# Mixture-of-experts stage with slots by place: small experts in 32 slots on four column quarters, a float32 gather, and biases added behind the transposes

## The chip, the core and the metric

The kernel runs on one core of one Trainium2 chip. The metric is the device time of one execution in microseconds (us), as the median of several runs; lower is better. One execution is also recorded by the hardware profiler, and its rows are what this document reads.

## The reference, cut to what matters

One layer of a decoder: a token mixer (three attention branches) and then a mixture of 32 experts, over 256 tokens of width 1024, all in float32. The change is in the experts alone. A router picks four experts for each token, and what is computed is

```python
logits = tok @ router_w + router_b
top_v, top_i = lax.top_k(logits, 4)
top_w = softmax(top_v)                       # combine[t, e]: weight or 0
for e in range(32):
    gu = tok @ w_gu[e] + b_gu[e]             # (256, 2048)
    gate = minimum(gu[:, 0::2], 7.0)
    up = clip(gu[:, 1::2], -7.0, 7.0)
    act = (up + 1.0) * (gate * sigmoid(1.702 * gate))
    out = out + combine[:, e:e + 1] * (act @ w_down[e] + b_down[e])
```

The kernel computes an expert only for the tokens that were routed to it. An expert has 2048 columns of gate and up weights and 1024 of down weights, 12 MB in float32, and all 32 are read from HBM once.

## The kernel before

Behind the token mixer the router's logits are turned and the four largest are taken. Then experts are sorted by their number of tokens. **Places**: experts 0 and 1 have places 0 and 1 (FIXED), so that their weights can be loaded ahead of the sort; the others follow by falling number of tokens. Places 2 to 7 are **wide** (up to 128 tokens, class `Wide`), all others **narrow** (up to 64, class `Narrow`). If some place holds more tokens than it has slots, a flag is set, and a branch behind the sweep (L1664) computes what was left out.

**Groups.** Experts come in groups of two members. For a group, `choose` (GpSimd) builds a 0/1 matrix `sel` of tokens by slots; `gather` multiplies tokens with it, so that X holds a group's tokens, transposed, in slots; `slots` turns `sel` into `selT` for the scatter; `weights` gathers the routing weight of each slot into `wsl`. The gather runs in fp32r on two halves of the tokens, `tokh` (rounded) and `tokl` (the rest): eight pieces for a group, four copied into X by ScalarE and four added by VectorE (L1244). `Group.plan` puts these pieces between the steps of the expert ahead.

**Steps.** `sweep` goes through 24 half-steps for each expert, in the order N N N N, then W N N N and so on (N narrow, W wide; the groups are a pair of narrow ones and a wide with a narrow one in turn). Matmuls of weights are float32 with 512 moving columns; X (or the activation) is the loaded operand. A wide expert uses 128 columns of the array. A narrow expert runs two matmuls on the two 64-column halves (`tile_position=(0, 64 * e)`): gate columns go to PSUM rows 0 to 63, up columns to 64 to 127. It does this for each half f of the hidden width: eight X steps of two halves of a copy each, with `part` behind steps 4 and 8, then four steps for down. `part` evicts the PSUM bank to `gu`, turns it by four transposes (L1425), and VectorE and ScalarE make the activation `an` (L1434 to L1440). Biases are added by one more matmul into the same bank, `bgu` times `pick` or `pickN`. `leave` scales y by `wsl` into `yh` and `yl`, and a scatter with `selT` adds it to four PSUM banks `acc`.

**Queues.** Order on TensorE, SyncE and GpSimd is that of the program; each engine goes on when its waits are fulfilled. All weights come over SyncE's queue (`Stream.raw`, L97): copies of 512 KB, 24 for an expert, into a ring of 35 slots (`Stream.slot`), of which 2 * PAIRS lie in a pool of large tiles that `tokh` and `tokl` share. A copy waits until the matmuls that read its slot's earlier content are done.

## Time and profile before

| | before |
|---|---|
| median of 3 runs | 1328.62 us (1326.39 to 1328.7) |
| profiled execution | 1328.49 us |
| its span | 1326.7 us |
| TensorE busy | 1283.1 us (97%) |
| VectorE, ScalarE, GpSimd busy | 33%, 22%, 7% |
| copies | 478.19 MB, mean 360 GB/s over the span |
| first and last copy of expert weights issued | 233.2 us, 1275.3 us |
| first expert matmul | 288.35 us |

The span is the time from the first to the last instruction of the profiled execution. PE is TensorE's matmul and PEld its weight load, DVE VectorE, ACT ScalarE, POOL GpSimd, SP SyncE, SPq the queue of copies that SyncE issues. Every float32 matmul stands in the trace as two passes with a weight load each. Matmul ends are modelled, so that the starts of weight loads are the better clock of TensorE.

### The profile page before, as it was taken

The numbers are of one execution on the slowest core, as the hardware profiler recorded it, in microseconds if no ns is written. First come the engines' busy times: TensorE is split into PE (matmuls) and PEld (weight loads), VectorE is DVE, ScalarE is ACT, GpSimd is POOL, SyncE is SP. The second block draws the span as 40 slices with busy tenths as digits, with TensorE's granted clock in tenths as the row PEclk, the third lists the DMA queues.
The fourth block names the chain that finished last, engine by engine and source line by source line (L and its number), as shares of the span: only waits on it lengthen the run. The fifth ranks groups of instructions, "written<-read, shape, count | busy, mean of one in ns | idle before, by whom it ended". The sixth has DMA issues, their size and how long they took to land. (4 is left out here: it accounts for less than half of the span.)

```text
span 1326.7 us, 18133 instructions
## 1 busy us (share of the span) xinstructions
PE 1283.1 (97%) x6198; PEld 653.3 (49%) x6198; DVE 433.6 (33%) x921; ACT 285.3 (22%) x552; POOL 97.5 (7%) x149
## 2 busy tenths in 40 slices
PE   6999999989999999999999999999999999999993
PEld 6889888863333443344335433543354335343431
DVE  7898788761131111211111121212121112111114
ACT  4555555341111011111111111011101110111112
POOL 0014621010000000000000000000000000000000
PEclk9999999999899999999999999999999999999997
DMA  9998787689999999999999999999999999899970
GB/s 364 352 333 287 267 275 271 222 318 395 408 408 409 409 409 407 406 404 344 411 408 409 319 402 409 408 329 409 409 399 337 409 408 400 315 409 409 407 287 34
DMA packets 134531, 478.19 MB, mean 360 GB/s; under 512 B 16557, under 2 KB 17130, under 8 KB 134432
## 3 DMA queue, kind: packets, MB, share of 16 engines
q1 hardware_dynamic: 132656, 471.66, 92.2%
q0 software_dynamic: 1632, 5.03, 1.1%
q8 instruction: 51, 0.84, 0.3%
q14 instruction: 48, 0.39, 0.1%
q10 hardware_dynamic: 144, 0.26, 0.1%
HBM read 475.82 MB, written 3.44 MB: 361 GB/s over the span
## 5 line engine op out<-in xcount | busy, mean ns | idle before, releaser
L192 PE MATMUL b<-raw,X 128*64 128x512 f32 (+1 forms) x2048 | 563.1, 599 | 0.0
L192 PEld LDWEIGHTS b<-raw,X 128*64 128x64 f32 (+1 forms) x2048 | 178.2, 146 | 268.4 <-issue 248.9
L192 PE MATMUL b<-raw,an 128*64 128x512 f32 (+1 forms) x1024 | 288.2, 606 | 1.2
L192 PEld LDWEIGHTS b<-raw,an 128*64 128x64 f32 (+1 forms) x1024 | 86.7, 147 | 131.8 <-issue 108.9
L192 PE MATMUL b<-hh,hi 128*128 128x256 f32 x336 | 97.9, 291 | 12.6 <-ACT hh L319 12.6
L1434 DVE TENSOR_SCALAR gm<-b 128x256 f32<-128x256 f32 x52 | 22.1, 424 | 234.6 <-PE b L1425 234.6
L192 PE MATMUL b<-hl,hi 128*128 128x256 f32 x336 | 95.9, 286 | 1.8 <-DVE hl L320 1.8
L192 PE MATMUL b<-hh,lo 128*128 128x256 f32 x336 | 95.5, 284 | 0.6 <-DVE lo L157 0.4
L1244 DVE TENSOR_TENSOR X<-b,X 128x256 f32<-128x256 f32 (+1 forms) x60 | 28.6, 477 | 167.8 <-PE b L192 167.8
L1315 DVE SCALAR_TENSOR_TENSOR yl<-b,wsl,yh 128x512 fp32r<-128x512 f32 x38 | 28.5, 751 | 165.8 <-ACT yh L1314 151.4
L1420 ACT ACTIVATE gu<-b 128x512 f32<-128x512 f32 x52 | 31.0, 597 | 199.3 <-PE b L192 199.3
L157 DVE TENSOR_TENSOR lo<-raw,hi 128x1024 fp32r<-128x1024 f32 (+1 forms) x58 | 69.5, 1212 | 11.4 <-ACT hi L146 9.4
L192 PEld LDWEIGHTS b<-hh,hi 128*128 128x128 f32 x336 | 64.0, 191 | 14.4 <-ACT hh L319 12.6
L146 ACT ACTIVATE hi<-raw 128x1024 fp32r<-128x1024 f32 (+1 forms) x58 | 59.8, 1047 | 31.7 <-PE b L192 23.0
L192 PEld LDWEIGHTS b<-hl,hi 128*128 128x128 f32 x336 | 63.7, 190 | 2.8 <-DVE hl L320 2.7
L192 PEld LDWEIGHTS b<-hh,lo 128*128 128x128 f32 x336 | 64.1, 191 | 1.3 <-DVE lo L157 1.0
L1172 POOL TENSOR_SCALAR sel<-cst,pq 128x128 fp32r<-128x128 f32 x48 | 28.1, 600 | 450.7 <-PE b L192 450.7
L1314 ACT ACTIVATE yh<-b,wsl 128x512 fp32r<-128x512 f32 x38 | 26.1, 687 | 153.1 <-PE b L192 153.1
L1242 ACT ACTIVATE X<-b 128x256 f32<-128x256 f32 (+1 forms) x60 | 25.5, 425 | 154.4 <-PE b L192 154.4
L1435 ACT ACTIVATE th<-gm 128x256 f32<-128x256 f32 x52 | 21.6, 416 | 137.9 <-DVE gm L1434 137.9
L192 PEld LDWEIGHTS b<-sel,tokh 128*128 128x128 f32 x240 | 34.0, 190 | 32.6 <-issue 32.0
L192 PEld LDWEIGHTS b<-sel,tokl 128*128 128x128 f32 x240 | 34.3, 193 | 27.7 <-issue 27.3
(321 smaller groups left out, 1242.9 us busy)
## 6 DMA issues: line engine op xcount, KB each, us to landing
raw<-in_wexp SPq DMA_DIRECT2D x768, 512.0 KB, 10.1
raw<-in_modg SPq DMA_DIRECT2D x32, 512.0 KB, 6.0
raw<-in_wmg SPq DMA_DIRECT2D x24, 512.0 KB, 9.5
raw<-in_moda SPq DMA_DIRECT2D x16, 512.0 KB, 8.3
raw<-in_cw SPq DMA_DIRECT2D x8, 512.0 KB, 9.2
raw<-in_wbr SPq DMA_DIRECT2D x8, 512.0 KB, 6.3
raw<-in_wout SPq DMA_DIRECT2D x8, 512.0 KB, 5.8
raw<-in_wg SPq DMA_DIRECT2D x8, 448.0 KB, 8.9
```

Of the source, the lines that this page charges most:

```text
L146: self.nc.scalar.activation(hi[:, :m], src, AF.Copy)
L157: self.nc.vector.tensor_sub(part[2][:, :m], src, hi[:, :m].bitcast(F32))
L192: PE.matmul(out, x, w, start=start, stop=stop, skip_group_check=True, **kw)
L1172: engine.tensor_scalar(sel[:, i].rearrange("p (r j) -> p r j", r=2), C("iota64")[:, None, :].to_broadcast([128, 2, 64]), src[:, i, p:p + 1 ...
L1242: ACT.activation(x, bv, AF.Copy)
L1244: V.tensor_add(x, bv, x)
L1314: return (yh, yl, lambda: ACT.activation(yh, y, AF.Copy, scale=wsl), lambda: V.scalar_tensor_tensor(yl, y, wsl, yh.bitcast(F32), op0=OP.mu ...
L1315: lambda: V.scalar_tensor_tensor(yl, y, wsl, yh.bitcast(F32), op0=OP.mult, op1=OP.subtract))
L1420: at(side, t, lambda: ACT.activation(gu, b, AF.Copy))
L1434: V.tensor_scalar(v(gm), zv[:, :, 0], 7.0, None, op0=OP.min)
L1435: ACT.activation(th[:, 0:256], gm[:, 0:256], AF.Tanh, scale=0.851)
```

## The change

- Three kinds of expert by place: places 2 to 8 wide (128 slots, one more than before), 0, 1 and 9 to 17 narrow (64), 18 to 31 **few** (32 slots, class `Few`). The groups are the two fixed, one narrow pair, and then seven times a wide with a narrow and a pair of few ones: the order is N N N N and seven times N W F F.
- `Few` runs four matmuls on the four 32-column quarters of the array: for the X steps, a quarter each for gate and up of either hidden half; for down, each quarter takes one half of the output for one half of the hidden width, and the scatter adds the two up. A step takes four copies; there are four X steps, one `part` behind them, and two down steps.
- The gather runs in float32 on `h2` itself: four pieces for a group, all copied by ScalarE. `tokh` and `tokl`, their splitting and the additions into X are gone; the ring has a fourth pair of slots (37 in all).
- Biases: `sort_biases` makes a table `biasT` by place (hidden unit on the partition) with 16 small matmuls once, and VectorE adds it to the turned values behind the transposes (`clipped`). The bias matmuls, `bgu`'s split, `pick` and `pickN` are gone. A wide expert now evicts to `gu` and turns gate and up, where it turned the product alone.
- Slot weights are gathered in float32 without a split.
- The flag also looks at place 18, and the branch behind the sweep handles the new kinds.

On TensorE, the second half of a narrow expert stands so before (`raw` is a weight slot, `cst` the identity; the first member after a wide expert):

```order
L192 MATMUL b<-raw,X 64x512 x12
L192 MATMUL b<-bgu,pickN 128x512
L192 MATMUL b<-raw,an 64x512 x4
L1425 MATMUL b<-cst,gu 128x128 x4
L192 MATMUL b<-raw,an 64x512 x12
```

On TensorE in the changed kernel, the second half of a few expert (first of its pair), with a piece of the gather (`sel`, `h`) and the scatter behind it:

```order
L190 MATMUL b<-raw,X 32x512 x16
L1285 MATMUL b<-cst,gu 128x128 x4
L190 MATMUL b<-raw,an 32x512 x16
L190 MATMUL b<-sel,h_3115 128x192 x4
L190 MATMUL b<-yh,selT 128x512 x2
L190 MATMUL b<-yl,selT 128x512 x2
```

Before, down matmuls of the first hidden half stood between the last X matmul and the transposes of the second half; now nothing stands between the last X matmul, the one set of transposes and the first down matmul of a few expert. The bias matmul is gone.

On VectorE, the activation of one narrow half before (its inputs come from the PSUM bank `b`):

```order
L1434 TENSOR_SCALAR gm<-b 128x256
L1436 TENSOR_SCALAR an<-b 128x256
L1437 SCALAR_TENSOR_TENSOR gm<-an,gm 128x256
L1440 SCALAR_TENSOR_TENSOR an<-th,gm 128x256
L1315 SCALAR_TENSOR_TENSOR yl<-b,wsl,yh 128x512
```

On VectorE in the changed kernel, the activation of a whole few expert:

```order
L1269 TENSOR_TENSOR gm<-b,biasT 128x256
L1271 TENSOR_SCALAR gm<-gm 128x256
L1269 TENSOR_TENSOR up<-b,biasT 128x256
L1273 TENSOR_SCALAR up<-up 128x256
L1369 SCALAR_TENSOR_TENSOR gm<-up,gm 128x256
L1372 SCALAR_TENSOR_TENSOR an<-th,gm 128x256
L1280 SCALAR_TENSOR_TENSOR yl<-b,wsl,yh 128x512
```

Six operations stand where four stood, the two additions from the table being new, and they stand once for a few expert, twice for a narrow one.

The diff, cut to its core:

```diff
-HALF = 64
 FIXED = 2
-WIDE = 8
+WIDE = 9
+NARROW = 18
 RAW_BUFS = 10
 LOW_BUFS = 4
 RAW_MORE = 11
-PAIRS = 3
+PAIRS = 4
 AHEAD = 4
...
-                tok = (tokh, tokl)[s]
...
+            def gather(self, t, c2):
+
                 b = ps()
+                n = self.members[0][1]
                 for c in range(2):
                     for i in range(2):
...
+                        sel = self.sel[:, i, 0:self.width]
+                        if len(self.members) == 2 and n < 128:
+                            sel = self.sel[:, i].rearrange("p (s j) -> p s j", s=2)[:, :, 0:n]
+                        mm(b[:, c * self.width:(c + 1) * self.width],
+                           h2[:, i, (2 * c2 + c) * 128:(2 * c2 + c + 1) * 128], sel, i == 0, i == 1)
+                at(side, t + 2, lambda: ACT.activation(
+                    self.X[:, 2 * c2:2 * c2 + 2, 0:self.width],
+                    b[:, 0:2 * self.width].rearrange("p (c w) -> p c w", c=2), AF.Copy))
...
+            def clipped(self, v, z, bias, gate):
+
+                shape = [128, z.shape[1], z.shape[2]]
+                V.tensor_tensor(v, z, bias[:, :, None].to_broadcast(shape), OP.add)
+                if gate:
+                    V.tensor_scalar(v, v, 7.0, None, op0=OP.min)
+                else:
+                    V.tensor_scalar(v, v, 7.0, -7.0, op0=OP.min, op1=OP.max)
 
...
+            def turned(self, gu):
+                z = ps()
+                for j in range(4):
+                    PE.transpose(z[:, j * 128:(j + 1) * 128], gu[:, j * 128:(j + 1) * 128], C("ident"))
+                return z
...
-                        mm(b, self.pick[:, up].to_broadcast([128, 128]), bgu[:, f * 512:(f + 1) * 512], False, True)
...
+                    z = self.turned(gu).rearrange("p (c s) -> p c s", c=4)
+                    bias = biasT[:, self.place, :, f, up]
+
+                    def gate():
+                        self.gm, self.th = t2k("gm", 1), t2k("th", 1)
+                        self.clipped(self.gm.rearrange("p (c s) -> p c s", c=4), z, bias, True)
+                        ACT.activation(self.th, self.gm, AF.Tanh, scale=0.851)
+
+                    def both():
+                        a = self.act[f] = t2k("an", 2)
+                        self.clipped(a.rearrange("p (c s) -> p c s", c=4), z, bias, False)
+                        V.scalar_tensor_tensor(self.gm, a, 1.0, self.gm, op0=OP.add, op1=OP.mult)
+                        V.scalar_tensor_tensor(a, self.th, 1.0, self.gm, op0=OP.add, op1=OP.mult)
+
+                    at(side, t + 2, both if up else gate)
+
+                at(turn, t, turned)
...
+        class Split(Expert):
...
+            def activation(self, z, m, slots, bias, t):
+
+                gm, th, up = t2k("gm", 1), t2k("th", 1), t2k("up", 1)
+                a = t2k("an", 2)
+                z = z.rearrange("p (m e s) -> p m e s", m=m, e=2)
+
+                def v(x):
+                    return x[:, 0:256].rearrange("p (m s) -> p m s", m=m)
+
+                def begin():
+                    self.clipped(v(gm), z[:, :, 0], bias[0], True)
+                    ACT.activation(th[:, 0:256], gm[:, 0:256], AF.Tanh, scale=0.851)
+                    self.clipped(v(up), z[:, :, 1], bias[1], False)
+                    V.scalar_tensor_tensor(gm[:, 0:256], up[:, 0:256], 1.0, gm[:, 0:256], op0=OP.add, op1=OP.mult)
+
+                at(side, t, begin)
+                at(side, t, lambda: V.scalar_tensor_tensor(a[:, 0:256], th[:, 0:256], 1.0, gm[:, 0:256],
+                                                           op0=OP.add, op1=OP.mult))
+                return a
...
-                        mm(b, self.G.pickN[self.slot], bgu[:, f * 512:(f + 1) * 512], False, True)
...
+        class Few(Split):
+
+
+            def step(self, h):
+                r, rest = divmod(h, 4)
+                if rest != 3:
+                    return
+                w = [W.use((self.key, 2 * r + e // 2), e % 2) for e in range(4)]
+                X = self.G.x(self.slot)
+                if r in (0, 4):
+                    self.b = ps()
+                for k2 in range(2):
+                    for e in range(4):
+                        c = 2 * (r % 4) + k2
+                        x = X[:, c] if r < 4 else self.act[0][:, 64 * c + 32 * (e % 2):64 * c + 32 * (e % 2) + 32]
+                        mm(self.b[32 * e:32 * e + 32], x, w[e](k2 * 512, 512), c == 0, c == (7 if r < 4 else 3),
+                           tile_position=(0, 32 * e))
+                if r == 3:
+                    self.part(self.b)
+                elif r == 5:
+                    self.y = self.b
+                    self.leave()
+
+            def part(self, b):
+                t = self.t0 + 16
+                gu = t2k("gu", 1)
+                at(side, t, lambda: ACT.activation(gu, b, AF.Copy))
+
+                def turned():
+                    self.act[0] = self.activation(
+                        self.turned(gu), 8, 32,
+                        [biasT[:, self.place].rearrange("p c f e -> p (c f) e")[:, :, e] for e in range(2)], t + 1)
+
+                at(turn, t, turned)
+
+        KIND = {128: Wide, 64: Narrow, 32: Few}
...
-        tokh = s8([128, 2, D], "tokh", F32R)
-        tokl = s8([128, 2, D], "tokl", F32R)
...
+        biasT = mp.tile([128, 32, 4, 2, 2], F32, name="biasT")
...
+        def sort_biases():
+            for e in range(2):
+                b = ps()
+                rows = slice(32 * e, 32 * e + 32)
+                for c in range(4):
+                    for f in range(2):
+                        k = 2 * c + f
+                        mm(b[:, 32 * k:32 * k + 32], bgu[rows, 512 * f + 128 * c:512 * f + 128 * c + 128], perm[rows],
+                           True, True, tile_position=(32 * e, 0))
+                at(side, 6, lambda e=e, b=b: V.tensor_copy(biasT[:, :, :, :, e].rearrange("p q c f -> p (c f) q"),
+                                                           b[:, 0:256].rearrange("p (k q) -> p k q", k=8)))
 
...
+        def slots_of(p):
+            return 64 if p < FIXED else 128 if p < WIDE else 64 if p < NARROW else 32
+
+        by = {n: [(p, n) for p in range(FIXED, NE) if slots_of(p) == n] for n in KIND}
+        groups = [G0, Group(pq, [by[64].pop(0), by[64].pop(0)])]
+        while by[32]:
+            groups.append(Group(pq, [by[128].pop(0), by[64].pop(0)]))
+            groups.append(Group(pq, [by[32].pop(0), by[32].pop(0)]))
+        assert not any(by.values())
```

## Rows read from the trace of the kernel before

**Rows 1.** The page: busy time, share of the span and count of each engine.

```profile
PE 1283.1 (97%) x6198; PEld 653.3 (49%) x6198; DVE 433.6 (33%) x921; ACT 285.3 (22%) x552; POOL 97.5 (7%) x149
```

**Rows 2.** Table by stretch: busy us per engine, granted clock, DMA share, GB/s.

```profile
290.00:1290.00 1000.00, 998.84 (x4225) 410.31 (x4223) 179.00 (x374) 129.86 (x245) 40.67 (x84) 1.00 1.00 391
420.00:460.00 40.00, 39.92 (x152) 17.33 (x148) 7.48 (x15) 4.11 (x8) 2.55 (x6) 1.00 1.03 409
740.00:780.00 40.00, 39.92 (x180) 15.42 (x180) 6.61 (x14) 5.18 (x9) 2.57 (x5) 1.00 0.96 347
```

**Rows 3.** Waits, copy queue (SPq) and weight loads (PEld): us in total, times, longest.

```profile
SPq L97 <- DMA raw<-in_wexp: 417.6, 562, 2.2
SPq L97 <- PE b L192: 156.0, 187, 3.9
...
PEld b L192 <- DMA raw<-in_wexp: 18.0, 64, 0.8
```

**Rows 4.** Timeline, PEld: first weight load of six experts; start us, us, instruction.

```profile
409.33 0.14 PEld L192 LDWEIGHTS b<-raw,X 128*64 128x64 f32 x2 [0.28 <-issue]
...
484.69 0.20 PEld L192 LDWEIGHTS b<-raw,X 128*64 128x64 f32 x4 [0.36 <-issue]
...
510.21 0.14 PEld L192 LDWEIGHTS b<-raw,X 128*64 128x64 f32 x2 [0.28 <-issue]
...
539.72 0.14 PEld L192 LDWEIGHTS b<-raw,X 128*64 128x64 f32 x2 [0.28 <-issue]
...
566.13 0.30 PEld L192 LDWEIGHTS b<-raw,X 128*128 128x128 f32 x2 [0.81 <-issue]
...
615.11 0.20 PEld L192 LDWEIGHTS b<-raw,X 128*64 128x64 f32 x4 [0.37 <-issue]
```

**Rows 5.** Timeline, PEld, of a narrow expert: a scatter, transposes, plain pairs.

```profile
616.02 0.14 PEld L192 LDWEIGHTS b<-raw,X 128*64 128x64 f32 x2 [0.29 <-issue]
...
618.59 0.14 PEld L192 LDWEIGHTS b<-raw,X 128*64 128x64 f32 x2 [0.29 <-issue]
...
625.82 0.14 PEld L192 LDWEIGHTS b<-raw,X 128*64 128x64 f32 x2 [0.28 <-issue]
626.77 0.42 PEld L1425 LDWEIGHTS b<-cst,gu 128*128 128x128 f32 x4 [0.81 <-issue]
...
627.84 0.14 PEld L192 LDWEIGHTS b<-raw,X 128*64 128x64 f32 x2 [0.29 <-issue]
...
629.13 0.14 PEld L192 LDWEIGHTS b<-raw,X 128*64 128x64 f32 x2 [0.28 <-issue]
629.56 0.14 PEld L192 LDWEIGHTS b<-raw,X 128*64 128x64 f32 x2 [0.28 <-issue]
```

**Rows 6.** Timeline of the same expert: last load, eviction gu, the VectorE chain.

```profile
624.14 0.19 PEld L192 LDWEIGHTS b<-bgu,pickN 128*128 128x128 f32 x1 [0.81 <-issue]
...
624.68 0.60 ACT L1420 ACTIVATE gu<-b 128x512 f32<-128x512 f32 x1 [1.70 <-PE b L192]
...
627.47 0.42 DVE L1434 TENSOR_SCALAR gm<-b 128x256 f32<-128x256 f32 x1 [2.29 <-PE b L1425]
...
628.84 0.43 DVE L1440 SCALAR_TENSOR_TENSOR an<-th,gm 128x256 f32<-128x256 f32 x1
```

**Rows 7.** Copies into raw from 290 us: count, ns, first and last issue; landing.

```profile
L97 SPq DMA_DIRECT2D raw<-in_wexp x739: 327/333/663, 289.9 to 1275.3; - x185
...
DMA to landing us min/median/max: 3.8/10.1/11.9
```

**Rows 8.** Timeline, PEld and ACT: last weight load of the experts, last eviction.

```profile
1303.77 0.14 PEld L192 LDWEIGHTS b<-raw,an 128*64 128x64 f32 x2 [0.29 <-issue]
...
1304.87 0.69 ACT L1314 ACTIVATE yh<-b,wsl 128x512 fp32r<-128x512 f32 x1 [4.70 <-PE b L192]
```

**Rows 9.** TensorE 32-row matmuls (timeline), then the table by stretch right after.

```profile
333.64 4.16 PE L192 MATMUL b<-raw,ppT 32*128 32x512 f32 x8
...
338.00:340.00 2.00, 2.00 (x8) 1.20 (x10) 0.42 (x1) 0.00 (x0) 0.00 (x0) 0.50 1.01 406
```

## The prediction

> **What bounds the kernel now.** I read the page first: TensorE is busy for 97% of the span [rows 1]. Busy is not the same as bound, so I went on to the table by stretch. While the experts run, the copies move 409 GB/s in the good stretches and 347 in a bad one, and 391 as a mean over 290 to 1290 us [rows 2]. So two resources are close to their limit together. The waits say which one ends last: the weight loads of TensorE waited for a copy only 64 times and 18.0 us in total, while the copy queue waited 156.0 us for TensorE to free a slot, in 187 waits [rows 3]. TensorE never starves; the copies are held up by it. (The 417.6 us in which the queue waits for an earlier copy is the ring at work, not a stall.)

> The starts of the experts confirm it [rows 4]. From 484.69 to 615.11 four experts take 25.5 us (narrow), 29.5 (narrow, with eight gathers for the next group), 26.4 (narrow) and 49.0 (wide): 130.4 us. The copies for four experts are 96 of 512 KB, and at 409 GB/s one takes 1.282 us, so 123.1. TensorE loses 7.3 us on the copies in each such period, six of which stand in the program. The **ceiling** of any gain here is therefore the copy stream: what it needs from the point where it is saturated, plus a tail.

> **The terms of the copy stream.** The median time is 1328.62 us; the profiled execution took 1328.49, its span 1326.7, so 1.8 us lie around the span. From 289.9 us on 739 copies are issued [rows 7]. The first 29 are not changed: they wait on work ahead of the experts. Run without a stall, 738 steps of 1.282 us put the last issue at 1236.0 instead of 1275.3; the median landing of 10.1 us, and about 1.5 us for the small copies of rows and biases between them, put the last landing at 1248. That is 39 us gained if TensorE keeps up. Then the tail. Before, the last landing (1275.3 + 10.1, so about 1285) finds TensorE with most of the last expert still to do; its final matmul begins at 1303.77 [rows 8]. In the changed kernel the last expert is a "few" one, whose last step (eight matmuls, four at a time) starts when its copies land. With 0.6 us to start, four passes, and the 1.1 us from the last pass to its eviction [rows 8], the eviction begins 3.0 us after the landing, at 1251 instead of 1304.87. What follows is not changed: 1326.7 - 1304.87 = 21.8 us. The span is then 1272.8.

> **Does TensorE keep up?** It has to do four experts (few, few, narrow, wide) in under 123.1 us.
> - Passes. Every f32 matmul is two passes over 512 columns. Two 64-column matmuls go side by side at 0.43 us a pair of passes [rows 5]. A narrow expert has 48 such pairs, 20.6 us. A few expert has 24 sets of four 32-column matmuls. The trace shows no quarter, so I bound it from both sides: 0.43 us a set (four truly side by side, 10.3 us an expert), 0.86 (two at a time, 20.6) or 1.72 (one at a time, 41). Below 0.43 nothing is possible, since each set streams 512 columns as the pair does. I take 0.43, the value of the nearest row, which shows that halves cost nothing extra.
> - Interruptions. Undivided work between column tiles delays the tiled stream: a scatter takes 618.59 - 616.02 less three normal pairs, 1.28 us; four transposes 0.73 [rows 5]. The first few expert of a pair carries the transposes of the choice, the slot weights (taken like transposes) and one late scatter of the wide one: 2.5 us. The second carries a scatter and four float32 gathers. Eight gathers made the second narrow expert 29.5 us instead of 25.5 less its 1.5 for choice and weights, so eight cost 5.5; the four new ones have as many passes (float32 takes two) and half the interruptions, and I take 4.8, between 2.7 and 5.5.
> - The new stall. A few expert does all its gate and up columns before anything is evicted, and its down matmuls then need all of it. TensorE waits for the eviction of `gu` (0.54 us after the last pass begins, and 0.60 long), the transposes (0.70 until VectorE begins) and a chain of six VectorE operations. Four of them took 1.80 us; the two additions from the bias table add their mean of 0.45 each [rows 5, 6]. Together 4.7 us where 0.43 was normal: 4.3. Queued behind it on TensorE are the down matmuls, and nobody else waits. It is paid only while TensorE is behind the copies; otherwise the next copies are not there yet either (four take 5.1 us).
> - Sum: first few 17.1, second 20.7. Narrow: 26.4 less two bias matmuls (about 0.6 each), plus 0.9 for two more VectorE operations ahead of its last down matmuls: 26.1. Wide: 49.0 less four bias matmuls of 0.43, plus eight more transposes (0.9) and some 0.5 for float32 gathers: 48.7. Together **112.6 us against 123.1**: TensorE has 10 us to spare where it lacked 7. The evictions (ScalarE for all X, the table's additions on VectorE) are hidden, VectorE and ScalarE being idle for most of the stage [rows 2].

> Can the ring cover the wide expert, which takes 18 us longer than its copies? At 409.33 TensorE starts the fifth expert [rows 4]; the copies of the fourth would have landed at 386, so it is 23 us behind. One narrow expert (-5) and the first wide one bring this to 36. The ring now has 37 slots (four pairs where there were three, and the two tiles `tokh` and `tokl` gone); less eight in flight (10.1 us of landing at 1.282), 29 slots hold 37 us. It just holds, and each later period is 10 us easier. From the second period on TensorE runs after the copies, and the last few expert is fed by them.

> **The clock in the tail.** That expert then waits for copies between steps. [...] At that level the last steps, their transposes and the scatter cost some 4.9 us more, so the span is 1272.8 to 1277.7. I take 1275, and with the 1.8 us **1277 us**.

> The rest costs nothing that shows: the table is built by 16 small matmuls after the fifth step of the first expert, when TensorE has 23 us of data in stock; the splits of `h2` and of the bias table, the additions into X and the copies of `pick` disappear from engines that had time.

> **Rivals.** *Quarters two at a time* (the slower side). If a set takes 0.86 us, each few expert costs 10.3 us more, the period is 133.2, and TensorE is the bound: 408 us to the end of the fourth expert (409.33 before, less bias matmuls), seven periods (932), 22 to the end: 1362, with the 1.8 about 1364. It turns from the forecast at 0.65 us a set (112.6 + 48 x 0.22 = 123.1) and is slower than before from about 0.75 on. One at a time would give some 1650. For it: no row shows four tiles. Against: halves run at full rate [rows 5]. [...]

> [...]

> *TensorE remains just behind*: sets of 0.65 to 0.75 us, a longer chain or partial lulls of the clock use up the 10 us, and the stalls of the queue shrink instead of vanishing: 1300 to 1325.

> *The change does not do what it says*: if a place held more tokens than its slots, the branch behind the sweep would run 34 expert passes, over 1000 us. Routing worked out from the reference's inputs gives 46 tokens at place 9 (64 allowed), 25 at place 18 (32), 18 and 2 for the fixed ones, 84 at most: it is not taken.

> **How the numbers follow.** Forecast (copies bound, 1266 to 1300) 0.80; just behind 0.09, of which 0.03 end within 0.2% of the time before, about what a measurement of this kernel can tell from no change; two or one at a time 0.06; clock low 0.04; branch 0.01. The range: the low end takes 411 GB/s (-5), a warm tail (-2) and the slots that come free earlier (-4), 1266; the high end adds a first period that stalls (up to 10), a low clock throughout the tail and insertions there (up to 13), 1300. Faster 0.86, same 0.03, slower 0.11.

> **What would show it.** Right: 409 GB/s without a hole from 290 to about 1240; waits of weight loads for copies of some 100 us or more, waits of the queue for TensorE near zero after the first periods; weight loads of 32 columns in sets of four 0.43 us apart; last expert copy issued near 1236; the granted clock partly at 0.50 in the few experts. Wrong: sets 0.86 us apart; holes in GB/s at each wide expert; a queue that still waits for TensorE; a second sweep behind the branch; a last landing before 1240 or after 1260.

## The result and the profile after

The changed kernel takes **1289.27 us** (median of four runs, 1288.51 to 1299.13) beside 1327.82 for the kernel before in the same comparison: a ratio of 0.9728, with a 95% interval of 0.968 to 0.9776. The forecast was 1277, with a range of 1266 to 1300. The side and the mechanism came out as forecast; the gain is 39 us where 52 were forecast. The profiled execution took 1289.56 us, its span 1287.8.

The page of the changed kernel answers [rows 1] with its line of busy times (share of the span, count), then the copies' GB/s in 40 slices of the span:

```profile
PE 1186.2 (92%) x6218; PEld 632.5 (49%) x6218; DVE 416.1 (32%) x902; ACT 276.5 (21%) x538; POOL 91.3 (7%) x123
...
GB/s 360 346 335 318 227 297 291 199 258 394 407 409 408 409 409 409 409 408 409 407 403 409 407 403 401 408 405 401 406 403 405 407 399 409 399 408 407 396 376 84
```

TensorE now has idle time, and the holes of the kernel before are gone. But the slices do not stay at 409: from the middle of the span (644 to 1191 us) they lie between 399 and 409. The tables by stretch (columns as in [rows 2]) and the waits (columns as in [rows 3]) of the changed kernel, from 290 to 1290 us for the waits:

```profile
420.00:460.00 40.00, 39.37 (x158) 17.72 (x157) 8.92 (x20) 5.09 (x10) 2.33 (x4) 1.00 1.03 409
...
540.00:1200.00 660.00, 618.32 (x2849) 271.87 (x2846) 110.37 (x236) 82.85 (x157) 24.40 (x42) 0.98 1.02 405
```
```profile
SPq L95 <- DMA raw<-in_wexp: 531.9, 712, 1.7
SPq L95 <- PE b L190: 25.7, 81, 1.3
...
PEld b L190 <- DMA raw<-in_wexp: 39.4, 86, 1.1
```

The copy queue's waits for TensorE fell from 156.0 us to 25.7, the longest from 3.9 us to 1.3; the weight loads' waits for copies rose from 18.0 us to 39.4 [rows 3]. The period of four experts, from the timeline of weight loads (start us, us, instruction), at its first repetition, before the copies limit it:

```profile
528.48 0.20 PEld L190 LDWEIGHTS b<-raw,X 128*64 128x64 f32 x4 [0.84 <-issue]
...
554.71 0.30 PEld L190 LDWEIGHTS b<-raw,X 128*128 128x128 f32 x2 [0.81 <-issue]
...
605.52 0.16 PEld L190 LDWEIGHTS b<-raw,X 128*32 128x32 f32 x8 [0.36 <-issue]
...
624.69 0.16 PEld L190 LDWEIGHTS b<-raw,X 128*32 128x32 f32 x8 [0.37 <-issue]
...
644.29 0.20 PEld L190 LDWEIGHTS b<-raw,X 128*64 128x64 f32 x4 [0.84 <-issue]
```

Narrow 26.2, wide 50.8, few 19.2, few 19.6: **115.8 us** where the four took 130.4 [rows 4]. Inside a few expert, sets of four 32-column loads follow each other 0.43 us apart:

```profile
1227.30 0.13 PEld L190 LDWEIGHTS b<-raw,X 128*32 128x32 f32 x4 [0.30 <-issue]
1227.73 0.13 PEld L190 LDWEIGHTS b<-raw,X 128*32 128x32 f32 x4 [0.30 <-issue]
1228.16 0.13 PEld L190 LDWEIGHTS b<-raw,X 128*32 128x32 f32 x4 [0.30 <-issue]
```

So four quarters run side by side at the pace of two halves, 0.43 us [rows 5]. Last, the copies (count, ns, first and last issue), and the end of the experts, which answers [rows 7] and [rows 8]:

```profile
L95 SPq DMA_DIRECT2D raw<-in_wexp x739: 327/333/816, 291.0 to 1252.5; - x185
```
```profile
1264.11 0.16 PEld L190 LDWEIGHTS b<-raw,an 128*32 128x32 f32 x8 [1.84 <-SPq L1674]
...
1266.05 0.69 ACT L1279 ACTIVATE yh<-b,wsl 128x512 fp32r<-128x512 f32 x1 [8.77 <-PE b L190]
```

The last copy is issued at 1252.5, 15 us after the forecast's 1237.5; from there the last eviction follows in 13.5 us, as forecast, and the end 21.8 us after it. **The whole miss lies in the copy stream**, and nothing in the lines above names its cause: TensorE hardly holds the queue, yet 738 steps took 1.303 us each instead of 1.282.

### The profile page after: what moved, and what is told of

It is laid out like the page before. It is cut to its first block, busy times and chain, and to the rows that moved or that the text cites. A ratio compares the mean times of both kernels' runs of the same rounds, so it can differ in the third digit from the quotient of the medians.

```text
span 1287.8 us, 17983 instructions
## 1 busy us (share of the span) xinstructions
PE 1186.2 (92%) x6218; PEld 632.5 (49%) x6218; DVE 416.1 (32%) x902; ACT 276.5 (21%) x538; POOL 91.3 (7%) x123
## 5 line engine op out<-in xcount | busy, mean ns | idle before, releaser
L190 PE MATMUL b<-raw,X 128*32 128x512 f32 (+2 forms) x2048 | 486.9, 600 | 1.4 <-DMA raw<-in_wexp 1.2
L190 PE MATMUL b<-raw,an 128*32 128x512 f32 (+2 forms) x1024 | 262.3, 661 | 41.7 <-issue 33.1
L190 PEld LDWEIGHTS b<-raw,X 128*32 128x32 f32 (+2 forms) x2048 | 157.9, 136 | 242.2 <-issue 210.6
L190 PEld LDWEIGHTS b<-raw,an 128*32 128x32 f32 (+2 forms) x1024 | 84.9, 145 | 179.4 <-issue 146.1
L1269 DVE TENSOR_TENSOR gm<-b,biasT 128x256 f32<-128x256 f32 (+1 forms) x50 | 25.0, 499 | 348.3 <-PE b L1285 348.3
L1170 POOL TENSOR_SCALAR sel<-cst,pq 128x128 f32<-128x128 f32 x60 | 35.0, 600 | 887.0 <-PE b L190 887.0
L190 PEld LDWEIGHTS b<-sel,h 128*128 128x128 f32 x512 | 72.6, 191 | 41.9 <-issue 41.9
L190 PE MATMUL b<-sel,h 128*128 128x64 f32 (+2 forms) x512 | 80.4, 301 | 0.2 <-DVE sel L1170 0.2
L1285 PEld LDWEIGHTS b<-cst,gu 128*128 128x128 f32 x256 | 29.1, 141 | 56.8 <-issue 32.4
L1285 PE MATMUL b<-cst,gu 128*128 128x128 f32 x256 | 40.4, 280 | 11.4 <-ACT gu L1466 11.4
## 6 DMA issues: line engine op xcount, KB each, us to landing
raw<-in_wexp SPq DMA_DIRECT2D x768, 512.0 KB, 10.1
```

What stands on the lines that cost most here:

```text
L190: PE.matmul(out, x, w, start=start, stop=stop, skip_group_check=True, **kw)
L1170: engine.tensor_scalar(out, iota, src[:, i, p:p + 1], None, op0=OP.is_equal)
L1269: V.tensor_tensor(v, z, bias[:, :, None].to_broadcast(shape), OP.add)
L1285: PE.transpose(z[:, j * 128:(j + 1) * 128], gu[:, j * 128:(j + 1) * 128], C("ident"))
```

## What stops the copies

The intervals between issues, read one by one, are 1.28 us, but once in 32 copies one is 2.0. The timeline of SyncE shows it as two rows of five copies each (start of the first, us until the end of the last, 0.33 us being an issue itself): four ordinary intervals, and four with one long one among them:

```profile
885.14 5.49 SPq L95 DMA_DIRECT2D raw<-in_wexp  x5
```
```profile
892.83 6.12 SPq L95 DMA_DIRECT2D raw<-in_wexp  x5
```

Four intervals of 1.28 are 5.1 us; the second row has 5.8. What comes late is the landing that SyncE waits for. In the DMA views of 878 to 882, 885 to 890 and 896 to 900 us the copies' median time to landing is

```profile
raw<-in_wexp SPq DMA_DIRECT2D x3, 512.0 KB, 10.1
```
```profile
raw<-in_wexp SPq DMA_DIRECT2D x4, 512.0 KB, 10.8
```
```profile
raw<-in_wexp SPq DMA_DIRECT2D x4, 512.0 KB, 10.1
```

Copies in flight at 894.3 us land 0.7 late. Eight are in flight (10.1 us of landing at 1.28 a copy), and each issue follows the landing of the eighth before it: by 0.02 to 0.46 us, median 0.12, at the 317 issues between 540 and 1200 us for which the trace tells that landing. The delay is not made up: behind the interval of 1.98 us the next ten are 1.25 to 1.29. At 894.3 one packet of another queue stands in the view of 894.2 to 894.5 us:

```profile
q14 instruction: 1, 0.01, 6.6%
```

It carries 8 KB of program (8192 bytes). A copy takes SyncE four instructions (an address, a wait, a move, the copy), so 32 copies are 128 instructions, and 8 KB are 64 bytes for each. Between 540 and 1200 us the trace has 16 such packets 127 to 130 instructions of SyncE apart, and at every one an interval of 1.82 to 2.09 us; at the six others of the same queue and size, which come in no step with SyncE, none is longer than 1.42. Another queue of program code, q8, sends 23 packets of 16 KB in this stretch (one at 895.4 us); at the 20 of them that stand away from SyncE's fetches no interval is longer than 1.73.

Three theories follow. **A**: the fetch of SyncE's own code delays its copies. **B**: the queue pauses after 32 copies, whatever SyncE executes. **C**: the forecast's mechanism is incomplete, and TensorE still holds copies back. Every experiment has its ratio from runs of the kernel before that were made beside it. The changed kernel's interval, 0.968 to 0.9776, is wide: e1 lies clear of it, e5 and e9 overlap with its upper end, so what tells there is the late landings in the traces, with the time as a second sign.

**e1, addresses known in advance.**

```diff
-                return A["wexp"][bass.ds(state["r"], 1), u][:, :, s * D:(s + 1) * D].rearrange("a p c -> p (a c)")
+                return A["wexp"][p, u][:, s * D:(s + 1) * D]
```

> The changed kernel, but the expert at place p is expert p, a number known when the program is written, so that SyncE computes no address for a copy (the experts that are multiplied are then not those that the tokens chose; all sizes stay). SyncE's part of a copy shrinks from four instructions to one or two. In the changed kernel a copy lands some 0.7 us late once in every 32 copies, when SyncE's queue of program code fetches 8 KB (32 copies of four instructions of 64 bytes are 8 KB). Theory A, the fetch of SyncE's code stops its copies for 0.7 us: the late landings now come every 64 copies or more, some 10 or fewer instead of 20 from 291 us on, and the time is 1281 to 1284 instead of 1289. Theory B, the queue itself pauses after 32 copies or 16 MB, whatever SyncE executes: still one in 32, 1288 to 1290. Theory C, the copies are late because TensorE still holds slots: no change, 1288 to 1290.

Measured: 1282.32 us (1281.76 to 1287.64), ratio to before 0.965 (0.9636 to 0.9664). SyncE executes 1.9 instructions a copy. The DMA view of 540 to 1200 us of the changed kernel, and the same of e1 (packets and mean rate; then the packets of queue 14):

```profile
DMA packets 73323, 267.39 MB, mean 405 GB/s; under 512 B 8142, under 2 KB 8142, under 8 KB 73278
...
q14 instruction: 22, 0.18, 0.1%
```
```profile
DMA packets 74009, 269.84 MB, mean 409 GB/s; under 512 B 8222, under 2 KB 8222, under 8 KB 73972
...
q14 instruction: 14, 0.11, 0.0%
```

Eight fetches less, and 409 GB/s, the forecast's figure, for 660 us. C is out, and B in its plain form too. The time came out where A put it, for more than A's reason: at the eight fetches of SyncE that are left no copy lands late by them (one long interval begins 1.5 us behind a fetch, at 1185.7 us, beside a packet of q8). The trace is that of the longest of the four runs, 1287.64 us. So either a fetch delays only copies addressed by a register, or the density of the program matters. e5 and e9 part these.

**e5, the expert's number loaded for every copy** (seven instructions instead of four, the copies unchanged).

```diff
-                if "r" not in state:
-                    state["r"] = rank_of(p)
-                return A["wexp"][bass.ds(state["r"], 1), u][:, :, s * D:(s + 1) * D].rearrange("a p c -> p (a c)")
+                def ap():
+                    return A["wexp"][bass.ds(rank_of(p), 1), u][:, :, s * D:(s + 1) * D].rearrange("a p c -> p (a c)")
+
+                return ap
...
-            src = self.raw(self.cur[s] if isinstance(self.cur, tuple) else self.cur[:, s * m:(s + 1) * m])[:, :m]
+            if isinstance(self.cur, tuple):
+                src = self.raw(self.cur[s]() if callable(self.cur[s]) else self.cur[s])[:, :m]
```

> The changed kernel, but SyncE loads the expert's number anew for every copy: three more instructions a copy (a load of 0.27 us, an address operation and a range assertion, some 0.6 us together, which lie in the 0.75 us that SyncE waits for a landing at each copy), so seven instructions instead of four. The copies themselves stay the same, addressed by a register. Theory A (SyncE's code fetch delays copies whose address comes from a register): a late landing every 18 copies instead of 32, some 32 instead of 18 from 490 us on, 10 us more: 1297 to 1301. Theory B (the queue pauses after 32 register-addressed copies, whatever else SyncE executes): 1288 to 1291.

Measured: 1300.43 us (1300.4 to 1301.84), ratio 0.9784 (0.9769 to 0.9799), 11 us above the changed kernel, as A says. Its view of 540 to 1200 us:

```profile
DMA packets 72486, 264.37 MB, mean 401 GB/s; under 512 B 8048, under 2 KB 8048, under 8 KB 72433
...
q14 instruction: 31, 0.25, 0.1%
```

The trace has a long interval at each of SyncE's fetches, now every 18 copies, and its 501 steps there took 1.314 us each. B is out: the copies are the same, and the pauses follow the instructions.

**e9, known addresses and the number loaded for nothing** (five instructions a copy).

```diff
-                return A["wexp"][p, u][:, s * D:(s + 1) * D]
+                def ap():
+                    rank_of(p)
+                    return A["wexp"][p, u][:, s * D:(s + 1) * D]
+
+                return ap
```

> The kernel of e1 (expert p at place p, addresses known when the program is written), but SyncE loads the number of the expert for every copy as in e5 and does not use it: five instructions a copy instead of two, no address from a register. e1 had eight fetches of SyncE's code between 530 and 1210 us and no copy that landed late at one of them. Theory A1, a fetch delays only copies whose address comes from a register: again no late landing at the fetches, 1281 to 1284. Theory A2, a fetch delays copies whenever SyncE's program is dense, so that it comes to the end of what is loaded: a late landing every 25 copies, some 23 from 490 us on, 1290 to 1295.

Measured: 1294.01 us (1291.48 to 1302.2), ratio 0.9751 (0.9712 to 0.9789). A2: the late landings are back, at each of the 19 fetches of SyncE's code between 540 and 1200 us, 25 to 27 copies apart, with addresses that no register holds.

```profile
DMA packets 73322, 267.38 MB, mean 405 GB/s; under 512 B 8143, under 2 KB 8143, under 8 KB 73276
...
q14 instruction: 23, 0.19, 0.1%
```

Shown, then: the late landings come with the fetches of SyncE's own code, at four, five and seven instructions a copy (between 540 and 1200 us at 16 of 16 in the changed kernel, at 19 of 19 in e9, every 18 copies in e5), and not at two (none at eight in e1); no run here has three.

The semaphore events of the traces show where the delay sits. A copy reports its landing by sixteen increments. In the changed kernel the last of them comes 10.12 us after the issue and the fifteenth after 6.85 (copy issued at 1047.6 us); the fetch at 1059.3 us moves the last one to 10.82, for the copies in flight, and leaves the other fifteen where they were, within 0.01. In e1 a fetch delays one increment too, by 0.7 to 0.8 us at the four fetches that stand alone (at 908.6 us from 6.73 to 7.56), but not the last one, which stays at 10.17. So in both traces a fetch delays one of the sixteen increments of the copies in flight, by 0.7 to 0.8 us, and the copies land late where that increment is the last. Why the last one is met in the changed kernel and not in e1 is not shown.

**e3, no wide experts** (theory C by itself).

```diff
-            groups.append(Group(pq, [by[128].pop(0), by[64].pop(0)]))
+            groups.append(Group(pq, [(by[128].pop(0)[0], 64), by[64].pop(0)]))
```

> The changed kernel with places 2 to 8 run as narrow experts too (their tokens past 64 are left out), so that TensorE needs some 25 us less for four experts and never holds a slot for long. Theory C (SyncE's 30 us of waits for TensorE are what the forecast missed): the copies reach 409 GB/s from 290 us on, the last one is issued at 1237 to 1240 and the time is 1274 to 1277. Theory A or B (the pause once in 32 copies): the last copy is issued at 1248 to 1252 and the time is 1284 to 1288.

Measured: 1287.69 us (1286.62 to 1288.6), ratio 0.9694 (0.968 to 0.9708). TensorE has some 25 us less to do in a period, and the time hardly moves. The timelines of SyncE from 540 to 1200 us, the changed kernel and e3, show the same pace, 659.0 us for 507 steps and 660.1 for 508, 1.300 us each:

```profile
540.91 659.34 SPq L95 DMA_DIRECT2D raw<-in_wexp  x508
```
```profile
539.79 660.41 SPq L95 DMA_DIRECT2D raw<-in_wexp  x509
```

The kernel before already had this pace between two holds by TensorE. Its timeline of SyncE from 416.7 to 583.4 us gives 166.5 us for 128 steps, 1.301 us:

```profile
416.77 166.83 SPq L97 DMA_DIRECT2D raw<-in_wexp  x129
```

## What the change's own parts are worth

**e6, without few experts** (float32 gather, biases behind the transposes and 37 slots stay).

```diff
-WIDE = 9
+WIDE = 8
...
-            return 64 if p < FIXED else 128 if p < WIDE else 64 if p < NARROW else 32
+            return 64 if p < FIXED else 128 if p < WIDE else 64
...
-        while by[32]:
-            groups.append(Group(pq, [by[128].pop(0), by[64].pop(0)]))
-            groups.append(Group(pq, [by[32].pop(0), by[32].pop(0)]))
+        for kind in "NWNWNWNWNWNWNNN":
+            groups.append(Group(pq, [by[128 if kind == "W" else 64].pop(0), by[64].pop(0)]))
```

> The changed kernel without its few experts: places 8 to 31 narrow, six wide, in the order of the kernel before (pairs of narrow ones between wide and narrow). What stays of the change is the float32 gather, the table of biases behind the transposes and the 37 slots. By the forecast's terms a period of four experts takes TensorE 1 to 2 us less than before (bias matmuls gone, gathers in fewer pieces, more transposes): 1316 to 1323. By the terms measured in the changed kernel (wide expert 50.8 instead of 49.0) these parts gain nothing: 1325 to 1332. Rival: the fourth pair of slots brings a good part of the gain: 1300 to 1315.

Measured: 1335.01 us (1331.33 to 1336.29), ratio 1.0041 (1.0028 to 1.0054). These parts gain nothing; alone they cost some 6 us. One period of its timeline:

```profile
676.87 0.14 PEld L190 LDWEIGHTS b<-raw,X 128*64 128x64 f32 x2 [0.29 <-issue]
...
703.46 0.30 PEld L190 LDWEIGHTS b<-raw,X 128*128 128x128 f32 x2 [0.81 <-issue]
...
807.96 0.14 PEld L190 LDWEIGHTS b<-raw,X 128*64 128x64 f32 x2 [0.28 <-issue]
```

A period is 131.1 us, 0.7 more than before, and the fifth expert begins at 414.8 us instead of 409.33 [rows 4]. What the bias matmuls took is outweighed by what came in their place. The whole gain of the change comes with the few experts, and with the order and the seventh wide place that belong to them; few experts without the other parts were not run.

**e10, each set of a few expert twice.**

```diff
+                    for e in range(4):
+                        c = 2 * (r % 4) + k2
+                        x = X[:, c] if r < 4 else self.act[0][:, 64 * c + 32 * (e % 2):64 * c + 32 * (e % 2) + 32]
+                        mm(self.b[32 * e:32 * e + 32], x, w[e](k2 * 512, 512), False, c == (7 if r < 4 else 3),
+                           tile_position=(0, 32 * e))
```

> The changed kernel with every set of four 32-column matmuls of the few experts issued twice (the sums are doubled). That costs TensorE 24 more sets of 0.43 us, 10.3 us in each few expert, and is what the rival of quarters that run two at a time would have cost. By the forecast's terms a period takes TensorE 112.6 + 20.6 = 133.2 us: 1364. By the period measured in the changed kernel when TensorE was not fed (117 us) it takes 137.8, so 408 + 965 + 22 and 2 outside the span: 1395 to 1400. If TensorE had more slack than either says, under 1350.

Measured: 1408.76 us (1406.88 to 1415.52), ratio 1.0611 (1.0578 to 1.0643). From its timeline, a narrow expert and the next period's:

```profile
828.97 0.20 PEld L190 LDWEIGHTS b<-raw,X 128*64 128x64 f32 x4 [0.84 <-issue]
...
965.40 0.20 PEld L190 LDWEIGHTS b<-raw,X 128*64 128x64 f32 x4 [0.84 <-issue]
```

The period is 136.4 us: 115.8 and 20.6, 48 sets of 0.43 us exactly. TensorE bounds throughout, as the copy queue's wait for it shows (290 to 1400 us), and this is what two quarters at a time would have cost.

```profile
SPq L95 <- PE b L190: 357.6, 228, 7.5
```

The total is 9 us above what I expected of this run: TensorE began the fifth expert at 413.4 instead of 408, and the last two few experts took 33.4 and 30.5 us at a clock that was partly 0.50.

**e11, 35 slots.**

```diff
-PAIRS = 4
+PAIRS = 3
```

> The changed kernel with three pairs of slots as before, 35 instead of 37. By the forecast the 37 slots just hold the 36 us by which TensorE is behind at the end of the first wide expert; with two slots less it holds 2.6 us less, once, at most: 1289 to 1293. Rival: each wide expert lets the copies stop (50.8 us against 31 of its copies), so that the ring matters in each of seven periods: 1300 or more.

Measured: 1289.73 us (1289.51 to 1295.61), ratio 0.9719 (0.9695 to 0.9743): the same as with 37. The fourth pair of slots brings nothing that shows.

**e7, a pair of few experts first.**

```diff
-        groups = [G0, Group(pq, [by[64].pop(0), by[64].pop(0)])]
-        while by[32]:
-            groups.append(Group(pq, [by[128].pop(0), by[64].pop(0)]))
-            groups.append(Group(pq, [by[32].pop(0), by[32].pop(0)]))
+        groups = [G0]
+        for kind in "FWFWFWNWFWFWFWF":
+            a, b = {"F": (32, 32), "W": (128, 64), "N": (64, 64)}[kind]
+            groups.append(Group(pq, [by[a].pop(0), by[b].pop(0)]))
```

> The changed kernel with the pair of narrow experts that follows the fixed ones moved to the middle, so that a pair of few ones comes there: TensorE, which starts 23 us behind the copies, then catches up by some 20 us before the first wide expert. Theory: TensorE sets the time up to the end of the first wide expert (copies 29 to 180 took 1.319 us each instead of 1.282, 5.6 us in all), so this gains 4 to 6 us: 1283 to 1286, and the runs that came out 10 us above the others (1299) vanish. Rival: the ring covers the first wide expert anyway: 1288 to 1290.

Measured: 1288.75 us (1287.4 to 1292.35), ratio 0.9702 (0.9685 to 0.9719): no gain. Copies 29 to 180 still took 1.313 us each (1.319 in the changed kernel), so that TensorE was not what slowed them there; this is the same 1.30 as everywhere, with the small loads.

**e4, small loads by GpSimd.**

```diff
-            nc.sync.dma_start(out=acc_bias[0][32:64], in_=A["bdn"])
+            POOL.dma_start(out=acc_bias[0][32:64], in_=A["bdn"])
...
-            nc.sync.dma_start(out=r[0:8], in_=A["rows"])
-            nc.sync.dma_start(out=r[8:9], in_=g2d)
+            POOL.dma_start(out=r[0:8], in_=A["rows"])
+            POOL.dma_start(out=r[8:9], in_=g2d)
```

> The changed kernel with the five small loads among the experts' copies (two rows loads twice, the down biases once) issued by GpSimd instead of SyncE. In the changed kernel the copy behind the last rows load is issued 3.85 us after the one ahead of it, 2.6 us more than the usual 1.28. Theory: the small loads stop SyncE's queue for these 2.6 us, the time falls by 2 to 3 us (1286 to 1287), and nothing from the first ones, which lie where TensorE still bounds. Rival: it is their bytes and rows that take the time, whoever issues them: 1289.

Measured: 1291.3 us (1287.59 to 1298.7), ratio 0.973 (0.9704 to 0.9756), its profiled run 1288.47. In the trace the stop of 3.85 us is gone and the last copy is issued 1.0 us earlier, but the runs spread over 11 us, so 2 us can't be told from none: inconclusive.

## A version that beats both

Fewer instructions per byte is what A asks for. **e2** fetches 1 MB at once where two slots lie side by side.

```diff
-RAW_MORE = 11
+RAW_MORE = 10
...
+    def two(self, cur):
+
+        self.count += self.count % 2
+        r = [self.slot() for _ in range(2)]
+        if self.pair is not None:
+            self.nc.sync.dma_start(out=self.pair, in_=cur[2])
+        else:
+            for s in range(2):
+                self.nc.sync.dma_start(out=r[s], in_=cur[s])
+        return r
```

> The changed kernel with copies of 1 MB where the ring has two slots side by side (28 of 36 slots; the other eight take 512 KB copies as before; the ring is one slot shorter). The bytes are the same, SyncE's instructions fall from 144 to 88 in a turn of the ring of 36 slots. Theory A (code fetch): a late landing every 52 slots instead of 32, 12 or 13 instead of 20, and 1283 to 1286. Theory B in bytes: one in 16 MB still, 1288 to 1290; theory B in copies: one in 32 copies, which are 52 slots here, so this run cannot tell it from A, but e1 can. Theory C (TensorE holds slots): the ring is shorter, 1289 to 1293.

Measured: 1282.93 us (1278.5 to 1290.73), ratio 0.967 (0.9647 to 0.9693). Its view of 540 to 1200 us has fewer fetches and the highest rate of all:

```profile
DMA packets 64061, 271.27 MB, mean 411 GB/s; under 512 B 5091, under 2 KB 5091, under 8 KB 56854
...
q14 instruction: 16, 0.13, 0.0%
```

At 0.7 us each, an estimate, six fetches less are worth 4 us of this. The rate lies above e1's 409, where no copy was late by a fetch of SyncE's; what gives the rest is not shown. Its packets are also fewer and longer (7207 of them of 8 KB or more, 37 in e1), and no run parts the two. **e8** adds the order of e7.

> Copies of 1 MB as in e2 and the order of e7 together, as a version meant to be better than both kernels: the late landings fall by 7 (5 us), the start by 5 us, and the stalls of the copies of 1 MB at the first wide expert go: 1270 to 1278. If the two gains are the same one (what is saved at the start is lost in the ring of 36 slots), 1280 to 1283.

Measured: 1278.91 us (1278.47 to 1288.44), ratio **0.9628** (0.9608 to 0.9648), some 10 us below the changed kernel and the lowest median here, though 0.9 us above the range that I expected. That it is faster than e2 is not shown: the lowest runs of the two are 1278.47 and 1278.5, and both spread over 10 us. Three runs of e8 lie within 0.5 us, two 6 and 10 above. The profiled run is the highest, 1288.44, and shows where its 10 us went; beside it the profiled run of e2, 1278.5. The tables of 1211 to 1254 us, e2 and then e8 (granted clock third from the right):

```profile
1211.00:1254.00 43.00, 36.18 (x233) 11.28 (x235) 5.30 (x14) 6.89 (x12) 0.00 (x0) 0.92 0.86 337
```
```profile
1211.00:1254.00 43.00, 39.44 (x187) 10.51 (x189) 3.11 (x8) 5.88 (x10) 0.00 (x0) 0.68 0.83 322
```

At a mean clock of 0.68 the last two few experts took 26.1 and 26.3 us instead of 21.6 and 20.3: 10.5 us, the whole difference. Where the granted clock was 0.50, sets of four stand 0.85 us apart (1225.27 and 1226.12 us) instead of 0.43. **e12** fills the lulls between the steps, which by its theory lower the clock.

```diff
+                if self.key in (NE - 2, NE - 1):
+                    z = ps()
+                    for _ in range(4):
+                        mm(z[:, 0:128], C("ident"), C("ident"), True, True)
```

> The kernel of e8 with four matmuls of the identity (128 columns, into a bank that nobody reads) behind each step of the last two few experts, some 0.9 us a step, in the 3 us that TensorE waits there for the next four copies. In the profile of e8 the granted clock was 0.50 for most of 1223 to 1254 us and these two experts took 52.4 us; in that of e2 they took 41.9. Theory (lulls between steps lower the clock there in some runs, and that is where runs come out up to 10 us above the others): no run over 1283, median 1277 to 1280. Rival 1 (the clock falls whatever fills the gaps): some runs at 1285 to 1290 as in e8. Rival 2 (the added matmuls delay the steps): all runs 3 to 10 us above 1278.5.

Measured: 1286.53 us (1285.31 to 1289.86), ratio 0.97 (0.9676 to 0.9724). The clock and the time came apart:

```profile
1211.00:1254.00 43.00, 40.45 (x281) 18.74 (x280) 3.10 (x8) 6.48 (x11) 0.00 (x0) 0.96 0.87 324
```

The clock is 0.96, and no time is gained: the two experts take 26.2 and 23.3 us with the added matmuls, 49.5 together beside 52.4 in e8's profiled run and 41.9 in e2's. The added matmuls delay the steps by most of what the clock could give back (7.6 of 10.5 us): rival 2, with one run (1289.86) above its range. That the lulls lower the clock is not shown: e2's profiled run has 0.92 without the added matmuls.

## Why the prediction was right, and where it missed

- **What bounds the kernel**: right. TensorE stood just behind the copies, with 130.4 us a period against 124.8 at their sustained pace, and at 115.8 the copies bound. e3 and e10 show both sides: taking work from TensorE changes nothing, adding 20.6 us a period makes it the bound.
- **The terms of the copy stream**: the step that was off, and it is one term. I took 1.282 us a copy from 409 GB/s, read in a stretch of 40 us [rows 2], and applied it to 738 steps; a term for the fetches of SyncE's code is missing. The sustained interval is 1.303: the code is fetched 23 times in that time, with a late landing at 21 of them, at 0.7 us each, 15 us, and 738 x 0.021 is 15.5. The count of issues over a long stretch of the kernel before would have told: 1.301. "About 1.5 us for the small copies" was 2.6 at the last of them. With the measured last issue (15.0 us later) the forecast's 1272.8 becomes 1287.8, the measured span; the 2.2 us taken for a low clock in the tail were not paid in the profiled run. No run shows the 4.9 us behind them, for last steps that all run at 0.50: the clock was 0.50 from 1258.5 to 1261.9 us, and the last down step, from 1264.11 on, ran at 1.00. That the time lies inside the range is luck in this respect: the range's upper part was for a first period that stalls, a low clock and insertions, and none of these took the 15 us.
- **Quarters at 0.43 us a set**: right to the row, by the timeline and by e10. With it the rival of two at a time fell, and its price was too low: 1364 where e10 measured 1409. The trace shows four column tiles at the pace of one pair of halves, 0.43 us.
- **TensorE's sum of 112.6**: 115.8, mis-sized without effect. Narrow was right (26.2 for 26.1). Wide was 50.8 for 48.7: in the weight loads, transposes take 1.5 us more, scatters 1.8 more and gathers 0.9 less than before, and the bias matmuls' 1.7 are gone. The first few expert took 19.2 for 17.1, since one of the four gather pieces stands there (1.5 us), and the second 19.6 for 20.7 for the same reason and because its scatter stands elsewhere. The four pieces take 6.0 us together, where 4.8 and at most 5.5 were taken. The stall, from the last X load to the first down load (613.40 to 618.42 us), is 5.0 for 4.7, whose parts as listed add up to 4.5.
- **The ring "just holds"**: right that it does, wrong that it needs 37; e11 lost nothing.
- **The rest "costs nothing that shows"**: right only in this kernel, where TensorE has 9 us to spare. Where it bounds, the parts other than the few experts cost 6 us (e6).
- **The tail**: right in sum, 13.5 us from the last issue to the last eviction and 21.8 behind it, but by two errors that cancel. The last copy's last increment comes at 1264.07 us, 11.6 after its issue instead of 10.1, and the eviction follows 2.0 us after it instead of 3.0. No run shows the "0.6 us to start" in the 3.0: the first weight load comes 0.04 us after that increment, at 1264.11.
- **The clock**: partly 0.50 in few experts, as forecast, in nine spells, 34 us together, between 500 and 1262 us of the profiled run. A low clock throughout the few experts, 0.04 in the forecast, did not come; in the profiled run of e8 the last pair was low for half of its time (27 of 52 us).
- **What would show it**: the queue's waits for TensorE did not go to zero (25.7 us) and the weight loads' waits for copies stayed under the 100 us named; e3 shows that the first meant no loss. One sign named for being wrong did come: the last landing was after 1260 us (1264.1), as the copies took 15 us longer.

## What to carry to other kernels

Where one queue carries the kernel, take the time of a copy from the issues over many copies, not from the GB/s of the best stretch (here 1.303 us beside 1.282), and look at the one interval that stands out (2.0 us among 1.28). In a stream of many small steps count the issuer's program as well, whose fetches cost some 15 us here: larger copies moved the same bytes with fewer instructions, and by the medians that was worth more (e2, 1282.93 us beside 1289.27) than an order of experts (e7, 1288.75) or two more slots (none: e11 has 1289.73 without them). A part that comes with a change can cost time and be hidden by the part that gains (some 6 us in e6), so run it alone.
